# Low-order weight tiles written in two halves, and two small tiles in the place of a finished one

## The chip, the cores and the metric

The kernel runs on one core of a Trainium2 chip. The metric is the device time of one execution in microseconds (us), the median of several runs; less is better. A core has five engines that work beside each other and wait for each other through semaphores: TensorE (PE) multiplies, VectorE (DVE) and ScalarE (ACT) work on tiles element by element, GpSimd (POOL) does little here, SyncE (SP) issues most DMAs. Each engine carries out its own instructions in the order in which they stand in its queue.

## The reference, cut to what matters

One decoder layer over 256 tokens of width 2048, in float32:

```python
h  = rms_norm(x, g_mix)
z  = h @ w_in                      # pool 512 | q-latent 512 | kv-latent 256 | rope key 64 | memory query 512
y  = concat(pool_mixer(z_pool), mla_mixer(z_q, z_kv, z_kr), memory_cross_attention(z_mq, mem)) @ w_o
x  = x + y
g, u = rms_norm(x, g_ffn) @ w_gate, rms_norm(x, g_ffn) @ w_up       # 2048 -> 5632
x  = x + (silu(causal_conv3(g)) * u) @ w_down
```

`memory_cross_attention` has 4 heads of 128 over 256 memory rows, `mla_mixer` 8 causal heads.

## The kernel before, in words

Float32 products are made of rounded float32 ("fp32r") matmuls: every operand is split into a high part (rounded) and a low part (the rest), and a product is high x high + high x low + low x high. ACT makes the high part of a weight tile (a CAST into `wh`), DVE the low part (a subtraction into `wl`); `split_w` does both. There are three buffers of each, so that the split can run up to three tiles ahead of PE.

`gemm_t` is one product of 2048 rows with 128 columns of weights, the weights as the stationary operand. It works in two chunks of 8 row blocks (c = 0 and c = 1), each with a tile of high and a tile of low weights of 128x1024. The order on PE is high 0, low 0, low 1, high 1, and the next product begins with its own high 0 again. So 16 high matmuls (512 columns wide, activations high and low side by side) alternate with 16 low ones (256 columns). `wl` is 64 elements longer than a tile needs, and the low tile begins `shift` elements into it: 48 elements (192 bytes) for c = 0, 16 elements (64 bytes) for c = 1. Bases of the buffers are all alike modulo 256 bytes.

The program has these stages: the projection of the memory (L137 to L139, to 51 us), the memory queries and the rope key (to 77 us), then the part that the change touches most: ten `gemm_t` products of the input projection, `z0` to `z5` (the latents, a loop over m) and four `pool_in(g)`, the latter mixed with `q_up` and `kv_up`. After these come MLA attention beside the output projection (to 288 us), 44 x 2 `gemm_t` products of gate and up (tiles `h`, to 773 us), and the down projection.

In z0 to z5 and pool_in(0) the four heads of the memory attention are worked in beside the products: after low 0 of each product, `between()` calls `mem_steps(m)`. For m = 0 that is `mq_done` (scales and transposes of the memory queries, and the row scale `rxb`); for the others `beside` lists which head does its scores (`score`: matmuls into PSUM, maxima on DVE, exponentials `p` on ACT, normalising on DVE), its transposes (`turn`: PE, then a copy `pT` on ACT), and its products with the values (`values`). At m = 6 `latent_scales` adds square roots. After each product `half_add` copies half of the sum out of PSUM (ACT, `hadd`), DVE adds the other half (`z`), and ACT and DVE make its square (`zs`, `zsq`) and its split (`zl`).

The order of instructions on an engine is set by a scheduler; an instruction that is issued through `keep(..., True)` is marked by `tc.keep_in_program_order`, which leaves the marked ones in the order in which the code issues them. In `gemm_t` the matmuls take the mark from the argument `kept` (True for z0 to z5 and pool_in(0), False in the other products); the two instructions of `split_w` do not, since `gemm_t` calls it without `kept`.

Of the kernel before, what the change touches and what calls it, by code (L numbers as in the profile page):

```python
# [25 lines left out]
ROPE = 64  # L26
# [11 lines left out]
HS = 1024  # L38
# [22 lines left out]
def layer(ctx, tc, xT_d, xn_d, memT_d, vec_d, tab_d, w_z_d, w_mqkr_d, w_q_d, w_kv_d, w_mem_d, w_pool_d, w_o_d,  # L61
          w_g_d, w_u_d, w_dn_d, out_d):
    nc = tc.nc

    const = ctx.enter_context(tc.tile_pool(name="const", bufs=1))
    stage = ctx.enter_context(tc.tile_pool(name="stage", bufs=1))
# [5 lines left out]
    def nm(s):  # L72
        uid[0] += 1
        return f"{s}_{uid[0]}"
# [13 lines left out]
    def keep(ins, on=True):  # L88

        return tc.keep_in_program_order(ins) if on else ins  # L90

    def split_w(raw, o, n, cut=HS, kept=False, shift=0):

        hi = stage.tile([P, HS], F32R, tag="wh", name=nm("wh"), bufs=3)
        lo = stage.tile([P, HS + 64], F32R, tag="wl", name=nm("wl"), bufs=3)[:, shift:shift + HS]
        for c in range(0, n, cut):
            e = min(n, c + cut)
            keep(nc.scalar.copy(hi[:, c:e], raw[:, o + c:o + e]), kept)  # L98
            keep(nc.vector.tensor_tensor(lo[:, c:e], raw[:, o + c:o + e], hi[:, c:e].bitcast(F32), op=ALU.subtract),  # L99
                 kept)  # L100
        return hi, lo

    def gemm_t(ps, raw, o, act, ks, first=True, last=True, kept=False, between=None):


        ks = list(ks)
        nk = HS // P
        cs = range(0, len(ks), nk)
        for c in cs:
            kc = ks[c:c + nk]  # L110

            hi, lo = split_w(raw, o + c * P, len(kc) * P, shift=16 if c // nk % 2 else 48)

            for low in ((False, True) if c // nk % 2 == 0 else (True, False)):
                for i, k in enumerate(kc):
                    w = (lo if low else hi)[:, i * P:(i + 1) * P]
                    keep(nc.tensor.matmul(ps[:, T if low else 0:2 * T], w, act(k)[:, 0:T] if low else act(k),  # L117
                                          start=first and c + i == 0 and not low,
                                          stop=last and c == cs[-1] and i == len(kc) - 1 and low == (c // nk % 2 == 0),
                                          skip_group_check=True), kept)  # L120
            if between is not None and c == 0:
                between()
# [50 lines left out]
    mp = mix.enter_context(tc.tile_pool(name="mix", bufs=1))  # L173
# [81 lines left out]
    ps = ps_aux()  # L255
# [25 lines left out]
    for c in range(KD // 2):  # L281
        raw = raw0 if c == 0 else load_w(w_mem_d[c], STG, HS if c == 1 else STG)
# [16 lines left out]
    ps = ps_aux()  # L299
# [62 lines left out]
    for c in range(KD // 2):  # L362
        raw = load_w(w_mqkr_d[c], 2 * 576)
        for i in range(2):
            hi, lo = split_w(raw, i * 576, 576)
# [9 lines left out]
            x_square(i)  # L375
        if c < 4:
            x_load()
    rxb = mp.tile([P, T], F32, name="rxb")

    def mq_done():  # L380

        x_rstd()
        for tt in range(NT):
            t = tok()
            nc.scalar.copy(t[:, 0:NH], pss[tt][0][:, :NH])
            nc.scalar.copy(t[:, NH:512], pss[tt][1][:, :512 - NH])
            nc.scalar.copy(kr[:, tt, :], pss[tt][1][:, 512 - NH:NH])
            head_sq(fmq3[:, tt], t[:].rearrange("p (h d) -> p h d", d=XD))
            nc.vector.tensor_scalar(fmq3[:, tt], fmq3[:, tt], rx2[:, tt:tt + 1], None, op0=ALU.mult)
            to_features(mqT, t, tt, XH, gqk[:, 1:2])  # L390
        rsqrt_(fmq, fmq, 1.0 / XD)
        for tt in range(NT):
            nc.vector.tensor_scalar(fmq3[:, tt], fmq3[:, tt], rx[:, tt:tt + 1], 1.0 / math.sqrt(XD),
                                    op0=ALU.mult, op1=ALU.mult)


        dx = tok()
        for tt in range(NT):
            nc.vector.tensor_scalar(dx[:, tt * P:(tt + 1) * P], identf[:], rx[:, tt:tt + 1], None, op0=ALU.mult)
        ps = ps_aux()  # L400
        nc.tensor.matmul(ps[:, 0:T], ones[:], dx[:, 0:T], start=True, stop=True)
        nc.scalar.copy(rxb[:], ps[:, 0:T])


    class Head:
# [75 lines left out]
    for m in range(6):  # L481
        raw = load_w(w_z_d[m], STG)
        if m in (1, 3):
            keep(nc.sync.dma_start(x1n[:, m // 2, :], xn_d[m // 2]))
        ps = ps_main()
# [3 lines left out]
        a = zs[:, m // 4, :]  # L489
        if m % 4 == 0:  # L490
            nc.scalar.activation(a, z[:], AF.Square)
        else:
            t = mp.tile([P, T], F32, tag="hadd", name=nm("zsq"), bufs=3)
# [21 lines left out]
    zp = mp.tile([P, 4, T], F32, name="zp")  # L515
    def pool_in(g):
        raw = load_w(w_z_d[6 + g], STG)
        ps = ps_main()
        gemm_t(ps, raw, 0, lambda k: xg[:, k, :], range(KD), kept=g == 0, between=lambda: mem_steps(6 + g))
        half_add(zp[:, g, :], ps)  # L520
        nc.vector.tensor_tensor(zp[:, g, :], zp[:, g, :], rxb[:], op=ALU.mult)


    def pool_mix():
# [60 lines left out]


    sskr, fk, fkn, fkr = sm(NT), sm(NT * H), sm(NT * H), sm(NT * H)
    krr = mp.tile([P, NT, 1, ROPE], F32, name="krr")
    for tt in range(NT):
        head_sq(sskr[:, tt:tt + 1], kr[:, tt:tt + 1, :])  # L590
        rotate(krr[:, tt], kr[:, tt:tt + 1, :], 1, tt, 1)
# [225 lines left out]
    for f in range(1, KF):  # L817
        pss = []
        for w in (w_g_d, w_u_d):
            raw = load_w(w[f], STG)  # L820
# [195 lines left out]
```

## Time and profile before

| what | value |
|---|---|
| median of 3 runs (lowest to highest) | 1008.01 us (1007.79 to 1008.3) |
| time of the profiled execution | 1008.52 us |
| its span, first to last instruction | 1006.7 us |
| PE, DVE, ACT busy | 1001.2, 751.4, 577.8 us |
| chain that ended last | PE 99% |
| granted TensorE clock | 1.000 |

A row of the timeline reads: start in us, duration in us, engine, line, operation, what it writes and reads, shapes, how many equal instructions it merges, and in brackets how long the engine had been idle and what ended that. Buffer numbers are left out in the profile, so that `wh<-wr` is any high tile. Matmuls are pipelined: a matmul's duration overlaps the next one, and the distance between starts is what PE needs for it.

### The profile page before, as it was taken

The numbers are of one execution on the slowest core, as the hardware profiler recorded it, in microseconds if no ns is written. First come the engines' busy times: TensorE is split into PE (matmuls) and PEld (weight loads), VectorE is DVE, ScalarE is ACT, GpSimd is POOL, SyncE is SP. The second block draws the span as 40 slices with busy tenths as digits, with TensorE's granted clock in tenths as the row PEclk, the third lists the DMA queues.
The fourth block names the chain that finished last, engine by engine and source line by source line (L and its number), as shares of the span: only waits on it lengthen the run. The fifth ranks groups of instructions, "written<-read, shape, count | busy, mean of one in ns | idle before, by whom it ended". The sixth has DMA issues, their size and how long they took to land.

```text
span 1006.7 us, 14129 instructions
## 1 busy us (share of the span) xinstructions
PE 1001.2 (99%) x5354; PEld 863.2 (86%) x5354; DVE 751.4 (75%) x1134; ACT 577.8 (57%) x853; POOL 18.5 (2%) x39
## 2 busy tenths in 40 slices
PE   9999999999999999999999999999999999999998
PEld 8898888888888888888888888888888888888886
DVE  6878689855677676776767677676767788888886
ACT  6778666544576555555555555555555565545553
POOL 1010000000000000000000000000000000010000
PEclk9999999999999999999999999999999999999999
DMA  9777344334665555554555555555555765576551
GB/s 361 260 243 297 129 165 178 128 146 145 210 208 210 179 197 193 184 208 172 205 184 195 194 184 209 174 203 185 191 200 201 263 214 191 205 275 212 206 209 42
DMA packets 31764, 200.17 MB, mean 199 GB/s; under 512 B 3664, under 2 KB 4176, under 8 KB 9808
## 3 DMA queue, kind: packets, MB, share of 16 engines
q1 hardware_dynamic: 28512, 189.04, 52.9%
q0 software_dynamic: 2752, 9.44, 2.6%
q8 instruction: 42, 0.69, 0.3%
q10 hardware_dynamic: 432, 0.79, 0.3%
q14 instruction: 26, 0.21, 0.1%
HBM read 195.06 MB, written 4.19 MB: 198 GB/s over the span
## 4 chain that ended last, share of the span: by engine, by line
PE 99%; DVE 0%; ACT 0%; issue 0%
PE psm L117 53%; PE psm L137 5%; PE psm L138 5%; PE psm L139 5%; PE psa L846 4%; PE psm L844 4%; PE psm L845 4%; PE psa L844 4%; PE psa L845 4%; PE psm L846 4%; PE psa L665 1%; PE psa L137 1%; PE psa L139 1%; PE psa L138 1%; PE psa L229 1%; PE psa L257 1%
## 5 line engine op out<-in xcount | busy, mean ns | idle before, releaser
L99 DVE TENSOR_TENSOR wl<-wr,wh 128x1024 fp32r<-128x1024 f32 (+2 forms) x338 | 392.3, 1165 | 63.7 <-ACT wh L98 58.7
L98 ACT CAST wh<-wr 128x1024 fp32r<-128x1024 f32 (+2 forms) x338 | 339.4, 1006 | 136.2 <-PE psm L138 47.3
L117 PE MATMUL psm<-h,wh 128*128 128x512 f32 x1408 | 336.8, 391 | 0.0
L117 PEld LDWEIGHTS psm<-h,wh 128*128 128x128 f32 x1408 | 257.7, 188 | 50.0
L117 PEld LDWEIGHTS psm<-h,wl 128*128 128x128 f32 x1408 | 176.1, 188 | 6.9
L117 PE MATMUL psm<-h,wl 128*128 128x256 f32 x1408 | 177.5, 278 | 0.0
L99 DVE TENSOR_TENSOR wl<-dn,wh 128x1024 fp32r<-128x1024 f32 x58 | 67.8, 1220 | 26.3 <-ACT wh L98 26.3
L98 ACT CAST wh<-dn 128x1024 fp32r<-128x1024 f32 x58 | 59.3, 1052 | 38.3 <-PE psm L845 21.7
L770 ACT COPY g<-psm 128x256 f32<-128x256 f32 x44 | 16.4, 372 | 88.7 <-PE psm L117 88.7
L771 DVE TENSOR_TENSOR g<-g,psm 128x256 f32<-128x256 f32 x44 | 18.5, 420 | 58.7 <-ACT g L770 58.7
L771 DVE TENSOR_TENSOR u<-u,psm 128x256 f32<-128x256 f32 x44 | 18.5, 421 | 52.8 <-ACT u L770 52.8
L781 ACT ACTIVATE gc<-gc 128x256 f32<-128x256 f32 x44 | 18.4, 419 | 63.9 <-DVE gc L780 63.8
L780 DVE SCALAR_TENSOR_TENSOR gc<-g,vec,gc 128x255 f32<-128x255 f32 x88 | 42.1, 478 | 0.3
L844 PE MATMUL psa<-wh,aT 128*128 128x512 f32 x104 | 40.5, 389 | 0.0
L845 PE MATMUL psa<-wh,aT 128*128 128x512 f32 x104 | 40.5, 389 | 0.0
L845 PE MATMUL psm<-wh,aT 128*128 128x512 f32 x104 | 40.5, 389 | 0.0
L846 PE MATMUL psa<-wl,aT 128*128 128x512 f32 x104 | 40.5, 389 | 0.0
L844 PE MATMUL psm<-wh,aT 128*128 128x512 f32 x104 | 40.5, 389 | 0.0
L846 PE MATMUL psm<-wl,aT 128*128 128x512 f32 x104 | 40.5, 389 | 0.0
L117 PE MATMUL psm<-xg,wh 128*128 128x512 f32 x160 | 39.9, 393 | 0.0
L137 PE MATMUL psm<-wh,cat 128*128 128x512 f32 x96 | 38.2, 398 | 0.0
L139 PE MATMUL psm<-wl,cat 128*128 128x512 f32 x96 | 37.4, 390 | 0.0
(227 smaller groups left out, 1393.9 us busy)
## 6 DMA issues: line engine op xcount, KB each, us to landing
wr<-in_w_g SPq DMA_DIRECT2D x44, 1024.0 KB, 4.8
wr<-in_w_u SPq DMA_DIRECT2D x44, 1024.0 KB, 4.8
wr<-in_w_dn SPq DMA_DIRECT2D x33, 1024.0 KB, 4.8
wr<-in_w_o SPq DMA_DIRECT2D x16, 1024.0 KB, 4.9
dn<-in_w_dn SPq DMA_DIRECT2D x11, 1024.0 KB, 4.9
wr<-in_w_z SPq DMA_DIRECT2D x10, 1024.0 KB, 5.5
wr<-in_w_mem SPq DMA_DIRECT2D x6, 1024.0 KB, 7.8
wr<-in_w_mqkr SPq DMA_DIRECT2D x8, 576.0 KB, 4.0
```

The source lines that it names most:

```text
L98: keep(nc.scalar.copy(hi[:, c:e], raw[:, o + c:o + e]), kept)
L99: keep(nc.vector.tensor_tensor(lo[:, c:e], raw[:, o + c:o + e], hi[:, c:e].bitcast(F32), op=ALU.subtract), kept)
L117: keep(nc.tensor.matmul(ps[:, T if low else 0:2 * T], w, act(k)[:, 0:T] if low else act(k), start=first and c + i == 0 and not low, stop=l ...
L137: keep(nc.tensor.matmul(ps, xh, hi[:, i, o], start=first and i == 0, stop=False), kept)
L138: keep(nc.tensor.matmul(ps, xl, hi[:, i, o], start=False, stop=False), kept)
L139: keep(nc.tensor.matmul(ps, xh, lo[:, i, o], start=False, stop=last and i == nk - 1), kept)
L771: nc.vector.tensor_tensor(t[:], t[:], ps[:, T:2 * T], op=ALU.add)
L780: nc.vector.scalar_tensor_tensor(gc[:, d:T], g[:, 0:T - d], v(w, f), gc[:, d:T], op0=ALU.mult, op1=ALU.add)
L781: nc.scalar.activation(gc[:], gc[:], AF.Silu)
L844: nc.tensor.matmul(ps, a[0], b[0], start=first, stop=False)
L845: nc.tensor.matmul(ps, a[1], b[0], start=False, stop=False)
L846: nc.tensor.matmul(ps, a[0], b[1], start=False, stop=last)
```

## The change

It does three things.

1. `gemm_t` calls a new function, `split_t`, in place of `split_w`. For c = 0 the low tile is written in two halves: matmuls 0 to 3 find their weights 192 bytes behind the base as before, matmuls 4 to 7 find theirs 64 bytes behind the base but for whole multiples of 256 bytes (the second half begins 544 elements behind the first). For c = 1 both halves are at 64 bytes and adjoin, as before. `wl` grows by 64 elements in each of three buffers, and with it every tile behind it moves by 768 bytes.
2. `split_t` gets `kept`, and hands it to `keep` for the CAST and the subtraction. In z0 to z5 and pool_in(0) these two are now marked, too.
3. `rxb` and `krr` become parts of one tile `late`, which takes the place of the sums of squares of the memory (`ssacc`), done by then.

```diff
-    def split_w(raw, o, n, cut=HS, kept=False, shift=0):
+    def split_w(raw, o, n, cut=HS, kept=False):
         hi = stage.tile([P, HS], F32R, tag="wh", name=nm("wh"), bufs=3)
-        lo = stage.tile([P, HS + 64], F32R, tag="wl", name=nm("wl"), bufs=3)[:, shift:shift + HS]
+        lo = stage.tile([P, HS + 128], F32R, tag="wl", name=nm("wl"), bufs=3)[:, 0:HS]
...
+    def split_t(raw, o, n, low, kept):
+        hi = stage.tile([P, HS], F32R, tag="wh", name=nm("wh"), bufs=3)
+        lo = stage.tile([P, HS + 128], F32R, tag="wl", name=nm("wl"), bufs=3)
+        d = n // 2 + (low[1] - low[0] - n // 2) % 64
+        lo2 = lo[:, low[0]:low[0] + 2 * d].rearrange("p (a n) -> p a n", a=2)[:, :, 0:n // 2]
+        half = lambda t: t.rearrange("p (a n) -> p a n", a=2)
+        keep(nc.scalar.copy(hi[:, :n], raw[:, o:o + n]), kept)
+        keep(nc.vector.tensor_tensor(lo2, half(raw[:, o:o + n]), half(hi[:, :n]).bitcast(F32), op=ALU.subtract), kept)
+        m = n // P
+        return ([hi[:, i * P:(i + 1) * P] for i in range(m)],
+                [lo2[:, i // (m // 2), i % (m // 2) * P:(i % (m // 2) + 1) * P] for i in range(m)])
...
-            hi, lo = split_w(raw, o + c * P, len(kc) * P, shift=16 if c // nk % 2 else 48)
+            hi, lo = split_t(raw, o + c * P, len(kc) * P, (16, 16) if c // nk % 2 else (48, 16), kept)
...
-                    w = (lo if low else hi)[:, i * P:(i + 1) * P]
+                    w = (lo if low else hi)[i]
...
-    rxb = mp.tile([P, T], F32, name="rxb")
+    late = mp.tile([P, 2, T], F32, tag="ssacc", name="late", bufs=1)
+    rxb = late[:, 0, :]
...
-    krr = mp.tile([P, NT, 1, ROPE], F32, name="krr")
+    krr = late[:, 1, 0:NT * ROPE].rearrange("p (t o d) -> p t o d", t=NT, o=1)
```

The number of instructions is the same on every engine. PE's order is the same but for one matmul of `q_up` that moves up by some places, and those of POOL and SP are the same. On ACT and DVE the order of z0 to pool_in(0) changes. Three places show it. In the names, the first number is the tile's.

ACT, at the middle of z0, before. The tiles wh_108 and wh_118 are those of z0 (c = 0 and 1; both casts stand further ahead), wh_124 and wh_132 those of z1, wh_139 the first of z2:

```order
L98 CAST wh_124_940<-wr_122_936 128x1024
L98 CAST wh_132_986<-wr_122_936 128x1024
L233 ACTIVATE mqT_109<-psa_112_879,small_82 128x4x128
L233 ACTIVATE mqT_109<-psa_115_893,small_82 128x4x128
L168 ACTIVATE small_82<-small_82,eps_72 128x8
L402 COPY rxb_839<-psa_117_906 128x256
L222 ACTIVATE hsq_189_1295<-kr_512 128x64
L222 ACTIVATE hsq_191_1305<-kr_512 128x64
L472 COPY hadd_121_930<-psm_107_846 128x256
L98 CAST wh_139_1018<-wr_137_1015 128x1024
L491 ACTIVATE zs_842<-z_120_929 128x256
L147 ACTIVATE zl_841<-z_120_929,vec_67 128x256
```

The same place with the change (L111 is the cast of `split_t`):

```order
L248 ACTIVATE mqT_109<-psa_112_879,small_82 128x4x128
L248 ACTIVATE mqT_109<-psa_115_893,small_82 128x4x128
L419 COPY late_839<-psa_117_906 128x256
L111 CAST wh_118_909<-wr_106_844 128x1024
L489 COPY hadd_121_930<-psm_107_846 128x256
L508 ACTIVATE zs_842<-z_120_929 128x256
L162 ACTIVATE zl_841<-z_120_929,vec_67 128x256
L111 CAST wh_124_940<-wr_122_936 128x1024
L440 ACT_TABLE_LOAD
L440 ACTIVATE p_127_963,st_128_964<-psa_126_960,st_128_964,small_82 128x256 x2
L440 ACTIVATE p_130_976,st_131_977<-psa_129_973,st_131_977,small_82 128x256 x2
L111 CAST wh_132_986<-wr_122_936 128x1024
```

The cast of z0's second tile moved behind the end of `mq_done` (`late` is the former `rxb`), that of z1's first tile from ahead of z0's copy out of PSUM (hadd_121) to behind z0's split, and that of z1's second tile behind the exponentials of heads 0 and 1. In z2 to z5 the first cast stands likewise behind the split of the product before, and the second behind the copy pT of that product's `turn`. pool_in(0)'s first cast stands ahead of z5's copy out of PSUM, its second behind the two square roots of `latent_scales`, and the first cast of `q_up(2)`, whose first matmul PE has there ahead of pool_in(0)'s low 1, behind that.

DVE, around z3, before (wl_166 and wl_174 are the low tiles of z4; head 2's maxima and normalising are st_155 and p_154):

```order
L473 TENSOR_TENSOR z_145_1065<-hadd_146_1066,psm_138_1017 128x256
L99 TENSOR_TENSOR wl_166_1156<-wr_163_1152,wh_165_1155 128x1024
L495 TENSOR_TENSOR zs_842<-zs_842,zsq_147_1069 128x256
L148 SCALAR_TENSOR_TENSOR zl_841<-z_145_1065,vec_67,zl_841 128x256
L99 TENSOR_TENSOR wl_174_1201<-wr_163_1152,wh_173_1200 128x1024
L145 TENSOR_TENSOR catm_840<-psa_152_1098,catm_840 128x256
L420 TENSOR_REDUCE st_155_1107<-psa_153_1103 128x1 x2
L421 TENSOR_TENSOR st_155_1107<-st_155_1107,small_82 128x2
L425 RECIPROCAL st_155_1107<-st_155_1107 128x2
L427 TENSOR_SCALAR p_154_1106<-p_154_1106,st_155_1107 128x256 x2
L473 TENSOR_TENSOR z_160_1143<-hadd_161_1144,psm_149_1077 128x256
```

With the change (wl_151 and wl_159 are the low tiles of z3 itself):

```order
L112 TENSOR_TENSOR wl_151_1079<-wr_148_1074,wh_150_1078 128x2x512
L160 TENSOR_TENSOR catm_840<-psa_152_1098,catm_840 128x256
L437 TENSOR_REDUCE st_155_1107<-psa_153_1103 128x1 x2
L438 TENSOR_TENSOR st_155_1107<-st_155_1107,small_82 128x2
L442 RECIPROCAL st_155_1107<-st_155_1107 128x2
L444 TENSOR_SCALAR p_154_1106<-p_154_1106,st_155_1107 128x256 x2
L112 TENSOR_TENSOR wl_159_1124<-wr_148_1074,wh_158_1123 128x1024
L490 TENSOR_TENSOR z_160_1143<-hadd_161_1144,psm_149_1077 128x256
L512 TENSOR_TENSOR zs_842<-zs_842,zsq_162_1147 128x256
L163 SCALAR_TENSOR_TENSOR zl_841<-z_160_1143,vec_67,zl_841 128x256
L112 TENSOR_TENSOR wl_166_1156<-wr_163_1152,wh_165_1155 128x2x512
```

Before, DVE made z4's low tiles ahead of head 2's softmax in z3; now z3's own second low tile stands behind that softmax, and z4's first behind z3's split.

PE, the same stretch with the change (before, the rows are the same with other line numbers):

```order
L132 MATMUL psm_149_1077<-xg_84,wh_150_1078 128x512 x8
L132 MATMUL psm_149_1077<-xg_84,wl_151_1079 128x256 x8
L458 MATMUL psa_152_1098<-pT_142_1043,mv_108 128x256
L460 MATMUL psa_152_1098<-pT_142_1043,mv_108 128x256
L467 MATMUL psa_153_1103<-mkT_110,mqT_109 128x256 x2
L450 MATMUL psa_156_1116<-identf_68,p_130_976 128x128 x4
L132 MATMUL psm_149_1077<-xg_84,wl_159_1124 128x256 x8
L132 MATMUL psm_149_1077<-xg_84,wh_158_1123 128x512 x8
L132 MATMUL psm_164_1154<-xg_84,wh_165_1155 128x512 x8
```

Nothing moved here: PE wants wl_159 right behind the transposes of head 1 (into psa_156), and wh_165 right behind z3's last matmul.

More of the change, by code (lines that the diff above doesn't have):

```diff
@@ L401, in mq_done @@
         nc.tensor.matmul(ps[:, 0:T], ones[:], dx[:, 0:T], start=True, stop=True)
-        nc.scalar.copy(rxb[:], ps[:, 0:T])
+        nc.scalar.copy(rxb, ps[:, 0:T])
     class Head:
@@ L520, in pool_in @@
         half_add(zp[:, g, :], ps)
-        nc.vector.tensor_tensor(zp[:, g, :], zp[:, g, :], rxb[:], op=ALU.mult)
+        nc.vector.tensor_tensor(zp[:, g, :], zp[:, g, :], rxb, op=ALU.mult)
     def pool_mix():
```

## The prediction

> **What bounds the kernel now.** I read the page first (busy time and the chain), then windows over the stage that the change reorders, then the timeline of that stage.
>
> ```profile
> PE 1001.2 (99%) x5354; PEld 863.2 (86%) x5354; DVE 751.4 (75%) x1134; ACT 577.8 (57%) x853; POOL 18.5 (2%) x39
> PE 99%; DVE 0%; ACT 0%; issue 0%
> ```
>
> PE is the bound from end to end, and the chain knows no other engine. So only two things can move the time: the pace of PE's own matmuls, and a wait that makes PE stop where it never stopped. This change touches both. The stage from z0 to pool_in(0), as windows (length, then busy time and instructions of PE, weight loads, DVE, ACT, POOL):
>
> ```profile
> 76.00:130.00 54.00, 54.00 (x316) 47.91 (x315) 40.03 (x97) 38.43 (x79) 0.00 (x0) 1.00 0.57 213
> ```
>
> PE works all 54.00 us. DVE and ACT are busy for 40.03 and 38.43 us, so their work must run ahead of PE to stay hidden; the last slack is in the order of their queues.
>
> **The pace of the low matmuls.** One gate product among the 88, at 507 us: the first row is the low tile of c = 0, the second that of c = 1, the third the high run that follows.
>
> ```profile
> 507.04 1.10 PE L117 MATMUL psm<-h,wl 128*128 128x256 f32 x8
> 507.98 1.07 PE L117 MATMUL psm<-h,wl 128*128 128x256 f32 x8
> 508.88 3.81 PE L117 MATMUL psm<-h,wh 128*128 128x512 f32 x16
> ```
>
> Starts are 507.98 - 507.04 = 0.94 us apart for eight matmuls (118 ns each), then 508.88 - 507.98 = 0.90 us (113 ns). The same instruction costs 5 ns less 64 bytes behind the base than 192 behind it. The change moves four of the first eight to 64 bytes: 4 x 5 = 20 ns a run at most, 88 runs in gate and up: 1.8 us. The wait of a matmul or two that a switch may need comes at the eighth matmul today and at the fourth then, so it is not paid twice; I take 1.6 us gained. The bounds: if a switch in the middle of a tile upsets the rhythm of the rest, the 12 matmuls behind it could go at the slower pace, 4 of them as today and 8 x 5 = 40 ns lost, 3.5 us lost in 88 runs; if the whole run went at the faster pace, 8 x 5 ns x 88 = 3.5 us gained.
>
> [...] The two rows above differ by the place of the weights alone, so I go by them.
>
> The subtraction in two halves has as many elements as before, and the 768 bytes move all later tiles by whole multiples of 256 bytes, at which the three `wl` buffers stood apart already: both at nothing (if such a move did matter, it would be in the bounds just given). What hides a slower subtraction in gate and up is that PE needs 5.5 us for a product in which DVE has two of them; without that cover it would cost its excess twice per product. The shared tile `late` is free long before it is written: nothing.
>
> **The new order in z0 to pool_in(0).** This is the large term. Before, both casts of a product stood far ahead of PE; with the change each stands behind work that itself waits for PE. z3 and z4 in the timeline of before, with PE, ACT and DVE, give all durations:
>
> ```profile
> 107.01 1.10 PE L117 MATMUL psm<-xg,wl 128*128 128x256 f32 x8
> 109.67 0.60 PE L433 MATMUL psa<-identf,p 128*128 128x128 f32 x4
> 110.03 1.19 PE L117 MATMUL psm<-xg,wl 128*128 128x256 f32 x8
> 110.31 0.58 ACT L436 COPY pT<-psa 128x512 f32<-128x512 f32 x1 [0.93 <-PE psa L433]
> 111.06 3.82 PE L117 MATMUL psm<-xg,wh 128*128 128x512 f32 x16
> 111.12 0.56 ACT L423 ACTIVATE p<-psa,st,small 128x256 f32<-128x256 f32 x1 [0.23 <-DVE st L421]
> 112.36 0.17 DVE L425 RECIPROCAL st<-st 128x2 f32<-128x2 f32 x1 [1.27 <-ACT p L423]
> 112.56 0.62 DVE L427 TENSOR_SCALAR p<-p,st 128x256 f32<-128x256 f32 x2
> 113.15 0.37 ACT L472 COPY hadd<-psm 128x256 f32<-128x256 f32 x1 [0.83 <-PE psm L117]
> 113.42 1.05 ACT L98 CAST wh<-wr 128x1024 fp32r<-128x1024 f32 x1
> 113.56 0.42 DVE L473 TENSOR_TENSOR z<-hadd,psm 128x256 f32<-128x256 f32 x1 [0.39 <-ACT hadd L472]
> 114.37 0.42 ACT L491 ACTIVATE zs<-z 128x256 f32<-128x256 f32 x1
> 114.51 1.22 DVE L99 TENSOR_TENSOR wl<-wr,wh 128x1024 fp32r<-128x1024 f32 x1 [0.53 <-ACT wh L98]
> 114.69 0.50 ACT L147 ACTIVATE zl<-z,vec 128x256 fp32r<-128x256 f32 x1
> 114.71 1.10 PE L117 MATMUL psm<-xg,wl 128*128 128x256 f32 x8
> 115.08 1.04 ACT L98 CAST wh<-wr 128x1024 fp32r<-128x1024 f32 x1
> ```
>
> A released engine starts 0.04 us after the end it waits for (hadd ends 113.52, z starts 113.56), and neighbours on ACT overlap by 0.1 (hadd 113.15 with 0.37, next 113.42).
>
> *Five ends of a product (z0|z1 to z4|z5).* The next high 0 now needs a cast that stands behind hadd, zs and zl. The run of 16 high matmuls from 111.06 takes to 114.71, 3.65 us; its first half belongs to the old product, so the next one would start at 111.06 + 1.83 = 112.89. hadd starts at 113.15, z ends at 113.98, zs can start at 114.02, zl 0.32 later (114.69 - 114.37), the cast 0.39 after that (115.08 - 114.69) at 114.73; it ends at 115.77, and PE is released at 115.81: 2.92 us of stop, five times, 14.6 us. z5's end is spared, since pool_in(0)'s first cast stands ahead of hadd.
>
> *z3 and z4, the middle.* Low 1 started at 110.03. Now its subtraction stands behind head 2's (3's) normalising, that behind its exponentials, these behind the cast, that behind pT. pT 110.31, cast 0.48 later at 110.79, exponentials 0.95 later at 111.74, RECIPROCAL 1.24 later (112.36 - 111.12) at 112.98, TENSOR_SCALAR at 113.18, subtraction at 113.72, ending 114.94; PE at 114.98: 4.95 us each, 9.9 us.
>
> *z2 and z5, the middle.* No scores there: pT (0.28 behind the old start of low 1), cast 0.48 later, 1.05 long, 0.04, subtraction 1.22, 0.04: 3.1 us each, 6.2 us.
>
> *z1, the middle.* The second cast stands behind four exponentials of heads 0 and 1.
>
> ```profile
> 87.03 1.89 PE L450 MATMUL psa<-mkT,mqT 128*128 128x256 f32 x8
> 88.57 1.27 PE L117 MATMUL psm<-xg,wl 128*128 128x256 f32 x8
> 88.86 1.08 DVE L420 TENSOR_REDUCE st<-psa 128x1 f32<-128x256 f32 x3
> 90.04 0.56 ACT L423 ACTIVATE p<-psa,st,small 128x256 f32<-128x256 f32 x1 [1.05 <-DVE st L421]
> 92.22 0.38 ACT L472 COPY hadd<-psm 128x256 f32<-128x256 f32 x1
> ```
>
> From the first maximum to the first exponential it is 1.18 us (88.86 to 90.04). The maxima of head 0 begin while the scores (87.03 to 88.57) still run, so I put the first exponential 0.5 us behind the last score; the four take 2.18 (90.04 to 92.22), cast 1.05, subtraction 1.22, two releases 0.08: 5.0 us.
>
> *z0, the middle.* The cast of its second tile stands behind all of `mq_done`.
>
> ```profile
> 80.56 0.23 DVE L389 TENSOR_SCALAR small<-small 128x4 f32<-128x4 f32 x1
> 81.31 1.29 PE L117 MATMUL psm<-xg,wl 128*128 128x256 f32 x8
> 81.60 1.26 ACT L233 ACTIVATE mqT<-psa,small 128x512 f32<-128x512 f32 x2
> 82.75 0.29 ACT L168 ACTIVATE small<-small,eps 128x8 f32<-128x8 f32 x1
> 82.94 0.36 ACT L402 COPY rxb<-psa 128x256 f32<-128x256 f32 x1
> ```
>
> The square root can start at 80.83, the mqT copies 0.19 later, `late` 1.15 after them (81.60 to 82.75) at 82.17, the cast 0.26 later at 82.43, with 1.05, 0.04, 1.22, 0.04 PE starts at 84.8 in place of 81.31: 3.5 us.
>
> *pool_in(0), the middle.* Its second cast stands behind the square roots, which need a table first:
>
> ```profile
> 123.94 1.28 ACT L168 ACT_TABLE_LOAD   x1
> 124.16 1.19 PE L117 MATMUL psm<-xg,wl 128*128 128x256 f32 x8
> 125.23 0.48 ACT L168 ACTIVATE small<-small,eps 128x2 f32<-128x2 f32 x2
> ```
>
> Roots end at 125.71, cast to 126.7, subtraction to 128.0 against 124.16: 3.8 us, less the 0.2 of the `q_up` matmul that now goes ahead: 3.6.
>
> Sum of the twelve stops: 14.6 + 9.9 + 6.2 + 5.0 + 3.5 + 3.6 = 42.8 us. After each stop the first weight load lies open, since no matmul runs beside it: 0.19 us by this row of the groups, 2.3 us in all.
>
> ```profile
> L117 PEld LDWEIGHTS psm<-h,wl 128*128 128x128 f32 x1408 | 176.1, 188 | 6.9
> ```
>
> **The clock.** PE now stops for 3 to 5 us twelve times. Before, it never stopped, so no row shows whether the clock then falls. The nearest rows are the program's start:
>
> ```profile
> 1.05 5.49 PE L257 MATMUL psa<-ones 128*128 128x128 f32 x24 [1.05 <-DVE eps L164]
> 6.19 0.77 PE L137 MATMUL psm<-wh,mg 128*128 128x512 f32 x1
> 7.43 0.40 PE L137 MATMUL psm<-wh,mg 128*128 128x512 f32 x1
> ```
>
> PE was busy from 1.05, and a 512-wide matmul took 0.77 us at 6.19 and 0.40 at 7.43: full speed came after some 6 us of work. A fall costs at most one work stretch again (high 0 and low 0: 1.83 + 0.94 = 2.8 us), so the term lies between 0 and 12 x 2.8 = 34 us. I take one fall, 2.8 us, near the lower end.
>
> [...]
>
> Against the profiled execution: 1008.5 + 42.8 + 2.3 - 1.6 + 2.8 = 1054.8 us. The median is 0.5 lower: 1054.3 us, 46.3 more than before.
>
> **The rivals.**
> - *Not slower: the casts stay hidden.* If the stops fell away because a cast that stands late is still early enough, only the low tiles' term would remain: 1008.0 - 1.6 = 1006.4 us, or 1004.5 with the bound of 3.5. It decides when the twelve stops sum to less than the gain, 0.13 us each. For it speaks ACT's 15 us of idle time in the window; against it that hadd at 113.15 waited for PE, and whatever stands behind it waits too.
> - *Half of the stops.* My chains add up releases, and scores, maxima and copies could overlap more than I allow. With the five ends at 2 us and the middles a third shorter, 10 + 0.67 x 28.2 = 29 us: 1037 us to 1040.
> - *The clock falls at most stops* and comes back late, as after 1.05: 8 to 12 falls at 2.8 in place of one, 20 to 31 us more: 1074 to 1085. For it speaks that 6 us of work were needed at the start and work stretches are 2.8 to 5 us; against it, that half of the time is still work.
> - *The low tiles fall out of rhythm:* + 3.5 in place of - 1.6, 5 us above my sum, inside the range.
>
> **How the numbers follow.** The forecast case (1044 to 1064) has 0.70, half the stops 0.12, the clock 0.14, no stops 0.04. The range, 1040 to 1074, leaves out the case without stops, most of the clock's and the lower part of the half's. A measurement here tells 0.2% (2 us) from no change. Slower by more than that: 0.96; the case without stops splits into 0.03 within 0.2%, and 0.01 faster.
>
> **What would show it.** In the profile after, the window from 76 us to the end of pool_in(0) should be some 99 us long in place of 54, PE busy about 55 to 60 of them, and the chain should name ACT and DVE for 3 to 5% of the span. PE should wait for `wh` five times for 2.9 us and for `wl` six or seven times for 3 to 5 us. In gate and up, eight low matmuls of c = 0 should take about 0.92 us from start to start in place of 0.94, c = 1 still 0.90. The clock should show 1.00 but for one short dip. I am wrong if PE is as busy there as before, if stops stand where I have none (pool_in(1) and on), or if the low tiles of c = 1 go at 118 ns.

## The result, and the profile after

The changed kernel takes 1075.4 us (median of 5 runs, 1074.2 to 1079.1) against 1008.0: a ratio of 1.068 (95% interval 1.066 to 1.070), 67.4 us more. The prediction was 1054.3 us, with a range up to 1074. The direction and the twelve stops were right, the terms for the clock and for the low tiles were not: 21 us are missing from the sum.

The execution that the profile shows took 1079.1 us, with a span of 1077.4 us against 1006.7 before. It is the longest of the five, which differ with their mean granted clock (0.972 in the two at 1079 us, 0.976 to 0.978 in the three at 1074 to 1075), so a difference taken from the profile is up to 4 us larger than one of the medians.

From the page after: busy times, the granted clock in 40 slices, and the chain.

```profile
PE 1031.6 (96%) x5354; PEld 885.1 (82%) x5354; DVE 753.9 (70%) x1134; ACT 578.3 (54%) x853; POOL 18.5 (2%) x39
PEclk9997777899999999999999999999999999999999
PE 95%; ACT 3%; DVE 1%; issue 0%; ACTq 0%
```

The span grew by 70.7 us, but PE's busy time grew by 30.4 (1031.6 - 1001.2), with the same 5354 matmuls. So 40.3 us are new idle time of PE, and for 30.4 us more PE is busy with the same matmuls. The second row says where most of those 30.4 are: in slices 4 to 8, some 80 to 215 us, the clock is granted at 0.7 to 0.8. The chain has PE for 95%, with ACT and DVE, at 0% before, for 4%.

What PE waited for between 70 and 210 us (waiting line, engine, tile and line waited for: us in total, times, longest us):

```profile
PE psm L132 <- DVE wl L112: 23.3, 6, 5.1
PE psm L132 <- ACT wh L111: 13.7, 5, 2.8
PE psm L152 <- ACT wh L98: 3.4, 1, 3.4
```

These are twelve stops, 40.4 us. Behind 210 us no wait of PE is listed at all.

What sets the rest: the same tile's first and last low matmuls in gate and up, before and after (duration minimum/median/maximum in ns, then first and last start).

```profile
L117 PE MATMUL psm<-h,wl x1408: 276/279/285, 290.7 to 772.8; 128*128 128x256 f32 x176
```

```profile
L132 PE MATMUL psm<-h,wl x1408: 279/281/285, 357.9 to 843.4; 128*128 128x256 f32 x176
```

The first of them starts 67.2 us later: that is all that z0 to pool_in(0) lost. From the first to the last it is 485.5 us in place of 482.1: gate and up lost 3.4 us where a gain of 1.6 was forecast. 67.2 + 3.4 = 70.6 of the 70.7 us.

### The profile page after: what moved, and what is told of

Its sections match the earlier page's. It is cut to its first block, busy times and chain, and to the rows that moved or that the text cites. A ratio compares the mean times of both kernels' runs of the same rounds, so it can differ in the third digit from the quotient of the medians.

```text
span 1077.4 us, 14118 instructions
## 1 busy us (share of the span) xinstructions
PE 1031.6 (96%) x5354; PEld 885.1 (82%) x5354; DVE 753.9 (70%) x1134; ACT 578.3 (54%) x853; POOL 18.5 (2%) x39
## 4 chain that ended last, share of the span: by engine, by line
PE 95%; ACT 3%; DVE 1%; issue 0%; ACTq 0%
PE psm L132 53%; PE psm L152 5%; PE psm L153 5%; PE psm L154 5%; PE psm L863 4%; PE psa L863 4%; PE psm L862 4%; PE psa L862 4%; PE psa L861 4%; PE psm L861 4%; PE psa L682 1%; ACT wh L111 1%; DVE wl L112 1%; PE psa L152 1%; PE psa L154 1%; PE psa L153 1%
## 5 line engine op out<-in xcount | busy, mean ns | idle before, releaser
L112 DVE TENSOR_TENSOR wl<-wr,wh 128x1024 fp32r<-128x1024 f32 x196 | 239.6, 1224 | 24.4 <-ACT wh L111 17.7
L111 ACT CAST wh<-wr 128x1024 fp32r<-128x1024 f32 x196 | 205.8, 1051 | 21.6 <-PE psm L132 10.7
L98 ACT CAST wh<-wr 128x1024 fp32r<-128x1024 f32 (+2 forms) x142 | 133.4, 942 | 114.0 <-PE psm L153 41.2
L99 DVE TENSOR_TENSOR wl<-wr,wh 128x1024 fp32r<-128x1024 f32 (+2 forms) x142 | 152.8, 1085 | 46.8 <-ACT wh L98 46.4
L132 PE MATMUL psm<-xg,wh 128*128 128x512 f32 x160 | 57.3, 515 | 13.7 <-ACT wh L111 13.7
L132 PEld LDWEIGHTS psm<-xg,wh 128*128 128x128 f32 x160 | 39.6, 258 | 25.2 <-ACT wh L111 16.8
L132 PE MATMUL psm<-xg,wl 128*128 128x256 f32 x160 | 29.9, 346 | 23.3 <-DVE wl L112 23.3
L132 PEld LDWEIGHTS psm<-xg,wl 128*128 128x128 f32 x160 | 28.1, 250 | 26.3 <-DVE wl L112 25.0
L861 PE MATMUL psa<-wh,aT 128*128 128x512 f32 x104 | 40.5, 389 | 0.0
L861 PE MATMUL psm<-wh,aT 128*128 128x512 f32 x104 | 40.5, 389 | 0.0
```

Of the source, the lines that this page charges most:

```text
L111: keep(nc.scalar.copy(hi[:, :n], raw[:, o:o + n]), kept)
L112: keep(nc.vector.tensor_tensor(lo2, half(raw[:, o:o + n]), half(hi[:, :n]).bitcast(F32), op=ALU.subtract), kept)
L861: nc.tensor.matmul(ps, a[0], b[0], start=first, stop=False)
```

## The experiments

I had two questions. First, the 67.2 us: the stops account for 40.4, so is the rest the clock, and why did it fall so often? Second, the 3.4 us: why did low tiles that were moved to the faster place become slower?

### One part at a time

**Layout without marks.** The changed kernel, with the casts and subtractions unmarked:

```diff
-            hi, lo = split_t(raw, o + c * P, len(kc) * P, (16, 16) if c // nk % 2 else (48, 16), kept)
+            hi, lo = split_t(raw, o + c * P, len(kc) * P, (16, 16) if c // nk % 2 else (48, 16), False)
```

> The change whole, but the casts and subtractions of gemm_t without the mark that keeps program order (on ACT and DVE the queues are again those of before). Theory: the twelve stops and the falls of the clock come from the marks alone, and what is left is the slower low tile of c = 1 in gate and up, 86 runs x 39 ns = 3.4 us: 1011.4 us, clock 1.00, PE never idle in z0 to pool_in(0). Rival: part of the loss comes from the shared tile or the halves (a wait for `late`, a longer subtraction): over 1015 us, with stops of PE left in z0 to pool_in(0).

Measured: 1011.45 us (1011.1 to 1011.8), ratio 1.0032 (1.0019 to 1.0045), clock 1.00. Gate and up in its trace:

```profile
L132 PE MATMUL psm<-h,wl x1408: 279/281/285, 289.9 to 775.3; 128*128 128x256 f32 x176
```

They last 485.4 us as in the changed kernel, and start no later than before. So the marks alone make everything ahead of 358 us, and the layout the 3.4 us behind it. PE waits for nothing between 70 and 210 us.

**Marks without layout.** The kernel before, with one argument more:

```diff
-            hi, lo = split_w(raw, o + c * P, len(kc) * P, shift=16 if c // nk % 2 else 48)
+            hi, lo = split_w(raw, o + c * P, len(kc) * P, kept=kept, shift=16 if c // nk % 2 else 48)
```

> The kernel before, with the mark on the casts and subtractions of gemm_t and nothing else. Theory: the change's loss less the 3.4 us of the low tiles, 1071 to 1076 us, with the same twelve stops of 40 us in sum and the low tiles of c = 1 at 113 ns. Rival: the stops need the other parts too: under 1060 us.

Measured: 1071.87 us (1071.6 to 1072.2), ratio 1.0631 (1.0613 to 1.0649), clock 0.976. The two parts add up: 63.9 + 3.4 = 67.3 of 67.4 us, which is closer than the changed kernel's own spread of 5 us lets one expect.

**The addresses without the switch.** The changed kernel without marks, both halves of the first low tile at 192 bytes; the larger `wl`, the moved tiles and the shared `late` stay:

```diff
-            hi, lo = split_t(raw, o + c * P, len(kc) * P, (16, 16) if c // nk % 2 else (48, 16), kept)
+            hi, lo = split_t(raw, o + c * P, len(kc) * P, (16, 16) if c // nk % 2 else (48, 48), False)
```

> The change without the marks and without the switch inside a tile: the longer wl, the moved tiles and the shared tile stay, but both halves of c = 0 stand 192 bytes behind the base, as before. Theory of the rhythm (the faster pace is caught only where the switch of place falls at the right matmul): the low tiles of c = 1 go at 113 ns again, 1008.0 us. Theory of the addresses (the moved tiles have lost the faster pace): 118 ns in all low tiles, 1011.4 us.

Measured: 1008.17 us, ratio 1.0001 (0.9991 to 1.0010). The 768 bytes by which the tiles move, the shared place and the subtraction written through `split_t` cost nothing. What remains for the 3.4 us is the switch of place after four matmuls.

### Where the switch falls

Three products of gate and up in the timeline before, in which each row is one run of matmuls:

```profile
595.04 2.01 PE L117 MATMUL psm<-h,wl 128*128 128x256 f32 x16
596.88 3.81 PE L117 MATMUL psm<-h,wh 128*128 128x512 f32 x16
600.54 2.01 PE L117 MATMUL psm<-h,wl 128*128 128x256 f32 x16
```

And after:

```profile
597.83 2.05 PE L132 MATMUL psm<-h,wl 128*128 128x256 f32 x16
599.72 3.81 PE L132 MATMUL psm<-h,wh 128*128 128x512 f32 x16
603.37 2.05 PE L132 MATMUL psm<-h,wl 128*128 128x256 f32 x16
```

From one low run to the next it is 5.50 us before and 5.54 after, and the whole 0.04 us is in the low run (2.01 and 2.05); 0.04 x 86 = 3.4 us (two of the 88 products are worked in pieces and not counted). Start by start, the trace before has eight distances of about 117.6 ns at 192 bytes, and from then on 113.4 at 64 bytes. After, all sixteen are about 118 ns, the twelve at 64 bytes too. So 64 bytes is not in itself the faster place: what decides is whether the run falls into the faster pace when it switches.

**Survey of the switch.** Marks off; from one group of four products to the next, the low run switches from 192 to 64 bytes after another number of matmuls (later groups try other pairs of places):

```diff
+    PLAN = [(8, 16), (1, 16), (2, 16), (3, 16), (4, 16), (5, 16), (6, 16), (7, 16), (0, 16), (4, 0), (4, 32),
...
-            hi, lo = split_t(raw, o + c * P, len(kc) * P, (16, 16) if c // nk % 2 else (48, 16), kept)
+            hi, lo = split_t(raw, o + c * P, len(kc) * P, low_of(c // nk % 2, len(ks)), False)
```

> The change without the marks, with another place for the low weights in every four products of gate and up: the switch from 192 to 64 bytes after 8, 1, 2, 3, 4, 5, 6, 7 and 0 matmuls, then after 4 matmuls to other places, then some without a switch inside the tile (where the subtraction is cut in two, DVE has one more instruction). Read by the distance of the starts in the 16 low matmuls of a run. Theory of the rhythm: before, the distances at 192 bytes repeat every three matmuls (117, 118, 118 ns), so the switch after 2 and 5 should catch the faster pace (113 ns behind it) as after 8 does, and after 1, 3, 4, 6, 7 not. Theory of the addresses: none catches it, after 8 neither. A third theory, that four matmuls at 64 bytes are too few to settle: all switches but that after 7 catch it, given eight more.

Measured: 1011.2 us in one run; its rows are what counts. Low runs that switch after eight, one, two, four and five matmuls, in this order:

```profile
308.64 2.01 PE L148 MATMUL psm<-h,wl 128*128 128x256 f32 x16
...
330.68 2.05 PE L148 MATMUL psm<-h,wl 128*128 128x256 f32 x16
...
352.77 1.98 PE L148 MATMUL psm<-h,wl 128*128 128x256 f32 x16
...
396.71 2.05 PE L148 MATMUL psm<-h,wl 128*128 128x256 f32 x16
...
424.30 2.00 PE L148 MATMUL psm<-h,wl 128*128 128x256 f32 x16
```

From the starts of its matmuls, the sixteen distances sum to:

| switch after | 0 | 1 | 2 | 3 | 4 | 5 | 6 | 7 | 8 |
|---|---|---|---|---|---|---|---|---|---|
| ns | 1887 | 1887 | 1821 | 1841 | 1887 | 1834 | 1854 | 1887 | 1848 |

After 2, 5 and 8 matmuls the run falls into 113.4 ns at once; after 3 and 6 some matmuls later (with a distance of 122 or 123 ns on the way); after 0, 1, 4 and 7 never. The pattern has a period of three (0 means no switch: all sixteen at 64 bytes, and slow). The expectation had 3 and 6 among those that never catch, and the third theory in it falls with 1 and 4. The change moved the switch from 8, which catches, to 4, which does not. No other pair of places in this survey was better than 192 and 64.

**The switch after two.** In all transposed products, marks off:

```diff
+        cut = 2 * P
+        at = lambda c: c + low[0] + ((low[1] - low[0]) % 64 if c >= cut else 0)
...
+        for u, v in ((0, n),) if low[0] == low[1] else ((0, cut), (cut, n)):
+            keep(nc.vector.tensor_tensor(lo[:, at(u):at(u) + v - u], raw[:, o + u:o + v], ...
```

> Marks off, and the low tiles of c=0 switch from 192 to 64 bytes after two matmuls in place of four, in every transposed product (two subtractions of 256 and 768 columns for the tile). Theory: what the low run costs is set by where in the repeating pattern of three matmuls the switch falls; after two it falls into step at once, and 16 matmuls take 1821 ns in place of the 1848 ns of the kernel before. At 86 such runs that is 2.3 us, so 1008.0 - 2.3 = about 1005.7 us. Rival: the extra subtraction of each product delays the tiles, or the survey's four runs were luck: 1008 us or more.

Measured: 1005.66 us (1005.3 to 1005.8), ratio 0.9976 (0.9965 to 0.9986); 2.3 us less than before, as expected. The additional subtractions (1234 instructions on DVE in place of 1134) cost nothing that shows. The survey's four runs were no luck.

**Survey of the ends.** The high run behind a low run starts slowly: distances of 232, 236, 229, 232 and 231 ns ahead of a steady 226.7. One group of the first survey, with its low tiles at 96 bytes, lacked that. So the second survey keeps the start and moves the last tiles, or other first tiles:

```diff
+    BASE = [48] * 2 + [16] * 14
+    PLAN = [BASE, BASE[:15] + [24], BASE[:14] + [24] * 2, BASE[:12] + [24] * 4, BASE[:15] + [8], BASE[:14] + [8] * 2,
+            BASE[:15] + [32], BASE[:14] + [32] * 2, BASE[:15] + [20], BASE[:14] + [20] * 2, BASE[:15] + [28],
...
+            [56] * 2 + [16] * 14, [0] + [16] * 15, ...
```

> Marks off, and the places of the 16 low tiles of each gate and up product vary from one group of four products to the next, all with the switch after two or the nearest like it: the last one, two or four tiles of the run at 96, 32, 128, 80, 112, 224, 0 or 160 bytes, or the first two at 160, 224, 208, 176 or 96. Theory: the low run of the groups that leave the end alone takes 1821 ns, and the 16-matmul high run behind it (3653 ns, its first five matmuls at 228 to 236 ns in place of 226.7) shortens where the last low tile lies as in the run of the survey that gave 3631 ns, at 96 bytes. Rival: the high run's slow start doesn't depend on the last place, and all groups give 3653 ns.

Measured: 1008.1 us in one run; again its rows are what counts. The group with the last tile at 80 bytes (20 elements), and the group with only the first at 0 bytes:

```profile
484.52 1.99 PE L153 MATMUL psm<-h,wl 128*128 128x256 f32 x16
486.35 3.79 PE L153 MATMUL psm<-h,wh 128*128 128x512 f32 x16
489.98 1.99 PE L153 MATMUL psm<-h,wl 128*128 128x256 f32 x16
...
682.29 1.98 PE L153 MATMUL psm<-h,wl 128*128 128x256 f32 x16
684.10 3.81 PE L153 MATMUL psm<-h,wh 128*128 128x512 f32 x16
```

The place I named, 96 bytes, gave part of it: a high run of 3636 ns in place of 3653. At 80 bytes it is 3631, and the product takes 489.98 - 484.52 = 5.46 us; the low run pays 8 ns for its last tile. With two tiles at 80 or 96 bytes the high run is back at 3650. The first tile at 0 bytes gives the shortest low run, 1813 ns. So the last places of a low run, and how many tiles stand there, set how the high run behind it starts, and both effects depend on exact places and counts.

**Both together.** First tile at 0 bytes, fourteen at 64, the last at 80, marks off:

```diff
-            hi, lo = split_t(raw, o + c * P, len(kc) * P, (16, 16) if c // nk % 2 else (48, 16), kept)
+        places = ([0] + [16] * 7, [16] * 7 + [20])
...
+            hi, lo = split_t(raw, o + c * P, len(kc) * P, places[c // nk % 2], False)
```

> Marks off; in every transposed product the first low tile of the 16 stands at 0 bytes, the next 14 at 64 and the last at 80 (four subtractions for the two tiles). Theory: the places found in the two surveys add up: the low run takes 1813 + 8 ns and the high run behind it 3631 ns, 5452 ns in place of the 5501 ns of the kernel before, times 86 = 4.2 us less: 1003.8 us, 1003.2 to 1004.6. Rival: the two don't add up, or the extra subtractions cost something: 1005.5 us or more.

Measured: 1003.69 us (1003.7 to 1004.0), ratio 0.9956 (0.9943 to 0.9970). This is the fastest version, 4.5 us below the kernel before as measured beside it (1008.16 us), and no wait of PE stands in its trace between 70 us and the end. Its rows:

```profile
602.60 1.98 PE L142 MATMUL psm<-h,wl 128*128 128x256 f32 x16
604.42 3.79 PE L142 MATMUL psm<-h,wh 128*128 128x512 f32 x16
608.05 1.99 PE L142 MATMUL psm<-h,wl 128*128 128x256 f32 x16
```

### Which mark makes the stops

The changed kernel with the casts marked and the subtractions free:

```diff
-        keep(nc.vector.tensor_tensor(lo2, half(raw[:, o:o + n]), half(hi[:, :n]).bitcast(F32), op=ALU.subtract), kept)
+        keep(nc.vector.tensor_tensor(lo2, half(raw[:, o:o + n]), half(hi[:, :n]).bitcast(F32), op=ALU.subtract), False)
```

> The changed kernel, but only the casts on ScalarE are kept in program order; the subtractions on VectorE are free as before. Theory (a stop comes from whichever of the two stands late, and both stand behind the memory's steps): the stops at the first high tile of z1 to z5 and the ones in mid product stay, shorter where only the subtraction stood late (z3 and z4, 4.7 us, to some 3 us), the clock still falls after most of them: 1062 to 1073 us. Rival (VectorE's order alone makes the stops, as the page's 23.3 us against 13.7 us of waits would suggest): six stops or fewer, 1035 us or less.

Measured: 1072.2 us (1071.1 to 1072.4), ratio 1.0634 (1.0619 to 1.0648), clock 0.977. Its waits of PE between 70 and 210 us:

```profile
PE psm L132 <- DVE wl L112: 19.7, 6, 5.1
PE psm L132 <- ACT wh L111: 13.7, 5, 2.8
PE psm L152 <- ACT wh L98: 3.4, 1, 3.4
```

All twelve stops are there, and 3.6 us shorter in sum (19.7 for 23.3): the subtractions' marks lengthen z3's and z4's middles (2.88 us each here, 4.71 with them) and do no more. The row "PE waits for DVE's wl" names the last link; what makes the stop is the late cast ahead of it, on ACT, and the marked subtraction adds to two of them. What marked subtractions alone would do was not tried.

### What the clock costs

The changed kernel around its first falls, as windows (length, then busy us and instructions of PE, weight loads, DVE, ACT, POOL; granted clock, DMA share, GB/s). In this trace the clock changes 24 times from 85.38 to 194.60 us, each time 3.41 or 6.83 us after the change before, so the windows are cut at steps of 3.41 us:

```profile
81.97:85.38 3.41, 0.86 (x7) 0.87 (x8) 1.87 (x6) 1.23 (x3) 0.00 (x0) 1.00 0.00 0
85.38:88.80 3.42, 3.42 (x11) 2.61 (x10) 0.00 (x0) 0.00 (x0) 0.00 (x0) 0.50 0.90 323
88.80:92.21 3.41, 0.71 (x4) 0.34 (x3) 1.31 (x3) 2.55 (x5) 0.00 (x0) 1.00 0.70 293
92.21:95.62 3.41, 3.41 (x11) 2.74 (x10) 0.81 (x1) 0.86 (x1) 0.00 (x0) 0.50 0.02 5
95.62:99.04 3.42, 2.54 (x15) 1.98 (x14) 1.58 (x5) 0.31 (x1) 0.00 (x0) 1.00 0.00 0
```

The window in which PE stops still runs at 1.00; the next one is granted 0.50, and holds the matmuls that PE had waited to run. After the 0.86 us of work in the first window the clock halves, after 3.42 it is back, after 0.71 it halves again; after 2.54 it stays. So the stops of 3.00 and 2.70 us, each mostly in one such window, were enough. One stop in the kernel with marks alone shows the other case, its timeline row first:

```profile
174.48 1.19 PE L117 MATMUL psm<-xg,wl 128*128 128x256 f32 x8 [2.88 <-DVE wl L99]
```

```profile
169.69:173.10 3.41, 1.91 (x13) 1.52 (x12) 0.42 (x1) 1.84 (x4) 0.00 (x0) 1.00 0.00 0
173.10:176.52 3.42, 2.04 (x13) 1.87 (x14) 2.36 (x2) 1.01 (x2) 0.00 (x0) 1.00 0.26 57
176.52:179.93 3.41, 3.41 (x20) 2.94 (x19) 1.31 (x3) 1.19 (x3) 0.00 (x0) 1.00 0.59 250
179.93:183.34 3.41, 1.98 (x15) 1.79 (x14) 0.72 (x4) 2.15 (x5) 0.00 (x0) 1.00 0.00 0
183.34:186.76 3.42, 1.50 (x6) 1.48 (x7) 3.03 (x7) 2.81 (x3) 0.00 (x0) 0.50 0.17 19
```

Its 2.88 us fall half and half into two windows, PE works 1.91 and 2.04 us of them, and the clock stays. So in these records the clock goes with PE's work in one window and not with the length of the stop: 2.88 us that lie in two windows left it up, 2.70 us that leave 0.71 us of work in one did not. The limit is not sharp: a window with 1.98 us was followed by half speed.

**Stops filled.** To take the clock's part away and leave the late casts, the changed kernel gets matmuls on a tile of zeros in the stops, 166 of them, which add nothing to the sums:

```diff
+                for _ in range(fill[1]):
+                    keep(nc.tensor.matmul(ps[:, 0:2 * T], zr[:], act(0), start=False, stop=False,
...
-        gemm_t(ps, raw, 0, lambda k: xg[:, k, :], range(KD), kept=True, between=lambda: mem_steps(m))
+        gemm_t(ps, raw, 0, lambda k: xg[:, k, :], range(KD), kept=True, between=lambda: mem_steps(m),
+               fill=(11 if m else 0, (12, 21, 12, 20, 20, 12)[m]))
```

> The changed kernel with its marks and places as they are, and in each of the twelve stops of z0 to pool_in(0) extra TensorE matmuls on a tile of zeros that add nothing to the sums (11 ahead of the first high tile of z1 to z5, 12 to 21 where the second block is awaited, 14 in pool_in(0)). The products still wait as long for their casts and subtractions; only TensorE is busy meanwhile. Theory (the clock falls because TensorE does too little in a window, and that costs some 27 us beside the stops themselves): the granted clock stays at 1.00 and the time is 1075.4 - 27 = about 1048 us, 1044 to 1054. Rival (the rest beyond the stops is not the clock but other waits that the marks make): 1065 us or more even with the clock at 1.00.

Measured: 1054.9 us (1054.7 to 1055.2), ratio 1.0465 (1.0449 to 1.0481).

```profile
77.00:200.00 123.00, 121.43 (x614) 99.02 (x613) 64.98 (x145) 55.60 (x104) 0.00 (x0) 1.00 0.32 115
```

The clock stays at 1.00 throughout, and 20.5 us of the changed kernel's time are gone. The expectation stood 7 us lower, and the run lies 0.9 us above its range. Had the extra matmuls outlasted the stops?

**Stops filled in part.** The same with 108 matmuls, so that PE stands some time in each stop:

```diff
-               fill=(11 if m else 0, (12, 21, 12, 20, 20, 12)[m]))
+               fill=(7 if m else 0, (7, 15, 7, 14, 14, 7)[m]))
```

> As the run with filled stops, with fewer matmuls of zeros (7 where there were 11 or 12, 14 or 15 where there were 20 or 21, 9 where there were 14), so that TensorE still stands some 1 to 1.5 us in each of the twelve stops and the extra matmuls never outlast a stop. Theory (what lowers the clock is how little TensorE does within one window of 3.41 us, with the limit between a share of 0.41, after which it always fell, and 0.60, after which it did not): the clock stays at 1.00 with some 15 us of idle left, and the time is the kernel before with the stops and the low tiles alone, 1008.0 + 40.4 + 3.4 = 1051.8 us, 1050 to 1054. Rival (any stop of about 1 us is enough to lower the clock): the clock is at half speed behind most stops, 1060 us or more.

Measured: 1055.0 us (1054.6 to 1055.4), ratio 1.0464 (1.0450 to 1.0478), clock 1.00. Its waits of PE between 70 and 210 us, and its low matmuls of gate and up:

```profile
PE psm L134 <- DVE wl L112: 8.5, 6, 1.6
PE psm L134 <- ACT wh L111: 5.6, 5, 1.1
PE psm L158 <- ACT wh L98: 1.2, 1, 1.2
```

```profile
L134 PE MATMUL psm<-h,wl x1408: 277/281/285, 333.9 to 819.3; 128*128 128x256 f32 x176
```

Twelve stops of up to 1.6 us remain, and the clock does not fall once, not even behind the window in which PE works least:

```profile
97.68:101.09 3.41, 1.79 (x12) 1.32 (x11) 1.96 (x4) 0.86 (x1) 0.00 (x0) 1.00 0.12 14
101.09:104.51 3.42, 3.40 (x15) 2.45 (x13) 0.71 (x2) 1.11 (x4) 0.00 (x0) 1.00 0.74 292
```

That any stop of a microsecond is enough is thereby excluded. The time is that of the fuller run, so the extra matmuls outlast nothing.

My expectation was 3 us too low, and not because the stops are longer here. From the end of PE's last own matmul ahead of a stop to the start of its next own one, the twelve sum to 40.4 us, as in the changed kernel, and each is the same to 0.1 us. The end of z0, with seven extra matmuls in the stop:

```profile
85.25 2.01 PE L134 MATMUL psm<-xg,wh 128*128 128x512 f32 x8
87.09 1.78 PE L127 MATMUL psm<-xg,zr 128*128 128x512 f32 x7
89.96 2.11 PE L134 MATMUL psm<-xg,wh 128*128 128x512 f32 x8 [1.08 <-ACT wh L111]
```

That is 89.96 - 85.25 - 2.01 = 2.70 us, and 2.70 in the changed kernel. What the expectation left out is what a stop costs beyond its idle time. Matmuls that follow each other overlap (2.01 us for eight that start 1.84 us before the next), and across a stop they do not (89.96 - 85.25 = 4.71 us is the full 2.01 and 2.70): counted from start to start, against the same two matmuls in the kernel before, the twelve stops are 43.1 us. Another 0.6 us lies in the matmuls right behind them: behind the changed kernel's first stop, still at full clock, the first two starts are 0.22 us apart and the next ones 0.12. The stage as a whole agrees: from the first low matmul of z0 (78.7 us, before 79.2) to the first of gate and up it is 333.9 - 78.7 = 255.2 us in place of 290.7 - 79.2 = 211.5, so 43.7 us more.

So the changed kernel's 67.4 us are, by the medians, 20.4 for the falls of the clock (1075.4 - 1055.0), 3.4 of low tiles, and 43.6 of stops at full clock (1055.0 - 1008.0 - 3.4). In the longer execution of its profile the clock's part is 67.2 - 43.7 = 23.5 us.

## Why the prediction was wrong, point by point

- *The twelve stops, 42.8 us, and 2.3 for open weight loads.* The stops are right in place, number and size: 43.1 us from start to start, as the prediction counts them, with the clock kept up. Three stops in the changed kernel's timeline, at the middle of z0, its end, and the middle of z2:

```profile
84.52 1.36 PE L132 MATMUL psm<-xg,wl 128*128 128x256 f32 x8 [3.00 <-DVE wl L112]
...
91.82 3.48 PE L132 MATMUL psm<-xg,wh 128*128 128x512 f32 x8 [2.70 <-ACT wh L111]
...
119.39 1.98 PE L132 MATMUL psm<-xg,wl 128*128 128x256 f32 x8 [2.88 <-DVE wl L112]
```

  Forecast were 3.5, 2.92 and 3.1 us. The brackets hold the idle time alone; from start to start at full clock the three are 3.44, 2.87 and 3.13, and z1's middle, forecast at 5.0, is 5.46. So stepping through the new order with durations of the old trace gave every stop to within 0.5 us. The 2.3 us for weight loads measured 0.6 (43.7 - 43.1). One place was off: the twelfth stop comes at the matmul of `q_up` that waits for its own cast (L152 in the waits above), not at pool_in(0)'s low tile.
- *The clock, 2.8 us.* This is the step that failed: 20.4 us by the medians, 23.5 in the profiled execution. The prediction took one fall, near the lower end of its 0 to 34 us; against more falls it held "that half of the time is still work". No run shows the term of one fall: the changed kernel's record of the clock has twelve falls to 0.50 between 85 and 195 us, one behind each stop, of one or two windows each, 58 us in all. The prediction looked at the mean over a stretch, but in this trace the falls go with one window of 3.41 us, and each of the twelve stops, 2.7 to 5.1 us long and nine of them shorter than a window, left one with 1.3 us of work or less. The price of a fall, at most 2.8 us by the prediction, was of the right kind: 20.4 / 12 = 1.7 us each, 23.5 / 12 = 2.0 in the profiled execution. The rival "the clock falls at most stops", 1074 to 1085, is what happened; it had 0.14. That its range holds the result is partly luck: it has 8 to 12 falls at 2.8 us that come back late. Twelve falls at 1.7 put the prediction's sum at 1054.3 - 2.8 + 20.4 = 1071.9 us, and the rest comes from the low tiles.
- *The low tiles, -1.6 us.* The sign was wrong: +3.4 us. This is the second step that failed. It read a pace off a place ("The same instruction costs 5 ns less 64 bytes behind the base than 192 behind it"), and its two rows differ "by the place of the weights alone" only if what ran ahead of them does not matter; sixteen matmuls all at 64 bytes go at 118 ns. The bound that the prediction gave for an upset rhythm, 3.5 us lost, is what happened, with all of the twelve matmuls behind the switch at 118 ns; the prediction had named that as a sign of being wrong.
- *The place of the weights, taken as the cause of the pace.* The experiments put the same kernel at 1011.5, 1005.7 and 1003.7 us by the places of the low tiles, with more subtractions on DVE in the faster ones and none that PE waits for; so in this kernel the place counts. Whether the weight load's own pace or the matmul's carries the difference is open.
- *The layout's other parts at nothing.* Right: 1.0001 with all of them.
- *What the profile should show.* Five waits for `wh` and six for `wl` came as listed, with the one of `q_up` as the twelfth, and the chain names ACT and DVE for 4% (3 to 5 forecast). The clock shows twelve dips where one was forecast. PE at 55 to 60 us of work in a window of 99 did not come, since the clock made its work longer: gate and up began 67.2 us late, not 45.

With the measured terms in its own sum, 1008.0 + 43.1 + 0.6 + 3.4 + 20.4 = 1075.5 us against the median of 1075.4. That is a check of the stops and the low tiles alone, since the clock's term is itself a difference of medians.

## What to carry to other kernels

Idle time on PE had a second price in this dense kernel: a stop that left 1.3 us of work or less in a 3.41 us window was followed by half speed in the next. By these runs a stop is costed as its own length, 0.3 us for what the overlap and the first matmuls behind it lose ((43.1 + 0.6 - 40.4) / 12), and 1.7 to 2.0 us for the clock, or it is filled so far that each window keeps well over half of its work (1.98 of 3.41 us was once too little). A mark that fixes the order of a cast is costed by walking the new queue with old durations, and that walk came within 0.5 us of each stop here; marking the casts alone made all twelve, even where the wait is booked on the subtraction behind the cast. A pace that follows a place in memory should be tested at the exact count and place that the change will use, before it is extrapolated.

## What was not expected of the hardware

- In the changed kernel between 75 and 195 us, all windows at full clock with PE at work for 1.26 us or less of 3.41 were followed by half speed (12 windows), and none with 2.54 us or more. In between, the records of other runs mix: windows with 1.79 us (stops filled in part), 1.91 and 2.04 us (marks alone) kept full speed, one with 1.98 (marks alone) did not. What the hardware counts inside a window is open. At half speed, the changed kernel's windows with 2.81 us of work or more were followed by full speed (12 windows), those with 2.74 or less by half speed again (5).
- With low tiles at 192 and 64 bytes, low matmuls (256 columns) go at 113.4 or 117.6 ns by the history of their weights' places, with a period of three matmuls in where a switch catches; other pairs of places gave up to 120 ns. Why three is open: no run separates the weight load from the matmul in this.
- The places of the last weights of one run set the pace of the first matmuls of the next: 3653 ns for sixteen of 512 columns behind a last tile at 64 bytes, 3631 behind one at 80 but 3651 behind two, 3690 behind two at 32 bytes.
